# Unread TensorE products put into five waits of a one-core fp32 transformer chain

## The chip, the cores and the metric

The kernel runs on one core of one Trainium2 chip, as one program with one launch. The metric is the device time in microseconds (us), the median of several executions. One further execution is recorded by the hardware profiler; all rows below are from that one.

## The reference

A first block and four layers work on x of 512 x 1024 in fp32, together with a context of 256 rows. Cut to what matters here:

```python
def first_block(x, p, ...):
    u = rms_norm(h, norm_mix_w[l])
    proj = u @ w_in[l]
    ...                                   # RG-LRU half ya, HGRN2 half yb
    h = h + jnp.concatenate([ya, yb], axis=-1) @ w_out[l]
    gate = jax.nn.sigmoid(rms_norm(h, ple_norm_w[l]) @ w_ple_gate[l] + b_ple_gate[l])
    h = h + gate * (p[l] @ w_ple_proj[l])
    return rms_norm(h, final_norm_w)

def second_block(x, c, ctx, ...):
    for i in range(4):                    # conv, RWKV, attention, conv
        shift, scale, gate = modulation(c, mod_w[i], mod_b[i])
        h = modulate(rmsnorm(x, norm_g[i]), shift[:, None], scale[:, None])
        ...                               # hc: the same for the context
        x = x + gate[:, None] * y         # y: the layer's mixer of h and hc
    return rmsnorm(x, final_g)

def rwkv_features(h, proj, with_out):
    xx = centred_shift(h) - h
    lerp = lambda n: h + xx * mu[n]
    k = lerp(2) @ w_k
    ...

def rwkv_readout(o, r, v, k_sum, g, r_k, ln_g, ln_b, w_o):
    ...                                   # group norm of o, bonus
    return (y * jax.nn.silu(g)) @ w_o
```

In the RWKV layer the features feed a recurrence over 768 rows (context, then x) in both directions, which the kernel computes in chunks of 64 rows.

## The kernel before, in words

Rows lie on the 128 partitions in tiles of 128; X holds 4 such tiles of x, XC 2 of the context. For a matrix product an operand is split into a high and a low part (`hi`, `lo`, or `whi`, `wlo` for weights), each in a reduced fp32 form, and three products are summed: hi·hi, hi·lo, lo·hi. ScalarE makes the high part of a weight (L170), VectorE the low part (L173). A norm makes tiles xn, TensorE transposes them against the identity (L261 in `normed_T`, L693 in the layers), and ScalarE reads the transposed tile with its scale and shift into h (L710). PSUM is in two pools: `pmm`, six banks named mm for sums, and `ptr`, two banks named tr for transposes.

The program is laid out ahead by a planner: it runs through the kernel's instructions in a simulated time, and so fixes the order of each engine's list. On the chip every engine works through its list in order, and waits on semaphores. Where the kernel says `manual_schedule`, the order is that of the program text; `high_priority` moves instructions forward in it.

Five places matter here. (1) The beginning: the input rows, the identity and the first vectors are loaded, `_load_cols` transposes the vectors (L157), `normed_T` makes four tiles xn (L256) and transposes them, and the first products with w_in follow (L199 to L202). (2) The end of the first block: `done_g` adds the bias to the gate's sum in PSUM (L556), takes the sigmoid of z in place (L557), multiplies z in place by the projection of p (L561) and adds it to X (L562); for the very last tile a small square root of one column of z (L560) loads ScalarE's table early. Norms of the result follow, and the first conv layer transposes with L693. (3) The entry of the RWKV layer: `lerped(first)` makes, for each of eight feature tiles k, the shifted difference xx (L1050), the interpolation l (L1041), and its halves lhi (L270, ScalarE) and llo (L273, VectorE), which the products L199 to L202 read. (4) The end of the recurrence: `chain_o` sums one chunk's outputs in two PSUM banks `s.ops` (L1459, L1466), ScalarE copies them to Os (L1469), a transfer writes them out (L1471), and the readout reads rows back into ro, norms them and transposes them (L1654). Pools are closed and opened between the two (`open_w(4)`). (5) The end of the RWKV layer: `linear_tm` of w_o (L218 to L220), whose results are added to X and XC (L721, L722), and then the attention layer's norm and its transposes (L693).

Of the kernel before, what the change touches and what calls it, by code (L numbers as in the profile page):

```python
# [10 lines left out]
F32 = mybir.dt.float32  # L11
F32R = mybir.dt.float32r
AF = mybir.ActivationFunctionType
# [5 lines left out]
P = 128  # L19
D = 1024  # L20
# [49 lines left out]
class K:  # L70
# [16 lines left out]
    def setup(self):  # L87
        nc, es = self.nc, self.es
        self.const = self.pool(es, "const")
        self.small = self.pool(es, "small", bufs=3)  # L90
        self.open_w(side="right")

        self.ident = self.const.tile([P, P], F32, name="ident")
        self.cols = self.const.tile([P, NCOL], F32, name="cols")
        self.eps6 = self.const.tile([P, 1], F32, name="eps6")
        nc.vector.memset(self.eps6, EPS)
        self.eps5 = self.const.tile([P, 1], F32, name="eps5")
        nc.vector.memset(self.eps5, 1e-5)
        self.inv_d = self.const.tile([P, P], F32, name="inv_d")
        nc.vector.memset(self.inv_d, 1.0 / D)  # L100
        self.eps12 = self.const.tile([P, 1], F32, name="eps12")
        nc.vector.memset(self.eps12, 1e-12)
        self.epsg = self.const.tile([P, 1], F32, name="epsg")
        nc.vector.memset(self.epsg, 256e-5)
        self.KC, self.KA, self.NK = KC_OFF, KC_OFF["ka"], KC_OFF["nk"]
# [19 lines left out]

    def open_ctx(self, **kw):
        return self.pool(self.ses, "streamc", **kw).tile([P, 2, D], F32, name="XC")

    def mm(self):

# [112 lines left out]
        return t  # L243


    def normed_T(self, X, gain, pool):

        nc = self.nc
        hi = pool.tile([P, KT, T], F32R, name="hT_hi")
        lo = pool.tile([P, KT, T], F32R, name="hT_lo")  # L250
        with self.tc.tile_pool(name="ntw", bufs=1) as work:
            rstd = self.rms_rstd(X, 4, work)
            xn = []
            for i in range(4):
                t = work.tile([P, D], F32, name="xn", bufs=4)
                nc.vector.tensor_scalar(t, X[:, i, :], rstd[:, i:i + 1], None, ALU.mult)  # L256
                xn.append(t)
            for k in range(KT):
                ps = self.ptr.tile([P, 512], F32, name="tr")
                for i in range(4):  # L260
                    nc.tensor.transpose(ps[:, i * P:(i + 1) * P], xn[i][:, k * P:(k + 1) * P], self.ident)  # L261
                g = self.col(gain, k)
                nc.scalar.activation(hi[:, k, :], ps, AF.Copy, scale=g)  # L263
                nc.vector.scalar_tensor_tensor(lo[:, k, :], ps, g, hi[:, k, :].bitcast(F32), ALU.mult, ALU.subtract)
        return hi, lo
# [9 lines left out]
    def first_block(self, X, XC):  # L275
        nc, ins = self.nc, self.ins
        with ExitStack() as es:
            big = self.pool(es, "fb")
            mix = big.tile([P, KT, T], F32, name="mix")
            with ExitStack() as es2:  # L280
                up = self.pool(es2, "fbu")
                with self.tc.high_priority(offset=10 * WPRIO):
                    uh, ul = self.normed_T(X, "norm_mix_w", up)
                with self.tc.tile_pool(name="colp1", bufs=1) as pool:
                    self._load_cols(pool, [(8, P)])
                self.silu_cols()
# [231 lines left out]
        with ExitStack() as es2:  # L518
            st = self.pool(es2, "ple")
            bg = self.bcast_row("bg", ins["b_ple_gate"].rearrange("o n -> (o n)"), st)  # L520
            nc.sync.dma_start(XC, ins["ctx_2"].rearrange("o (t p) n -> p (o t) n", p=P))
            p = st.tile([P, 4, 256], F32, name="p")
            nc.sync.dma_start(p, ins["p"].rearrange("o b (t q) n -> q (o b t) n", q=P))
            ph = st.tile([P, 2, T], F32R, name="ph")
            pl = st.tile([P, 2, T], F32R, name="pl")
            for k in range(2):
                ps = self.ptr.tile([P, 512], F32, name="tr")
                for i in range(4):
                    nc.tensor.transpose(ps[:, i * P:(i + 1) * P], p[:, i, k * P:(k + 1) * P], self.ident)
                nc.scalar.activation(ph[:, k, :], ps, AF.Copy)  # L530
                nc.vector.tensor_tensor(pl[:, k, :], ps, ph[:, k, :].bitcast(F32), ALU.subtract)
            pp = st.tile([P, 4, D], F32, name="pp")
            w_pp = ins["w_ple_proj"].rearrange("o k n -> (o k) n")
            for nh in range(2):
                self.linear_tm(w_pp, nh * 512, lambda k: ph[:, k, :], lambda k: pl[:, k, :], TILES,
                               lambda j, t, ps, nh=nh: nc.scalar.activation(pp[:, j, nh * 512:(nh + 1) * 512], ps, AF.Copy),
                               kts=2)
            gh, gl = self.normed_T(X, "ple_norm_w", st)

            rsc, rs1, rs2 = [self.const.tile([P, 4], F32, name=n) for n in ("rsc", "rs1", "rs2")]  # L540
            for t in range(2):
                junk = st.tile([P, D], F32, name="junk")
                nc.scalar.activation(junk, XC[:, t, :], AF.Square, scale=1.0 / 32.0, accum_out=rsc[:, t:t + 1])
            self.rsqrt(rsc[:, 0:2], rsc[:, 0:2], self.eps6)


            fw = self.bcast_row("fw", ins["final_norm_w"], st)
            s1, s2 = [st.tile([P, 4, 2], F32, name=n) for n in ("s1", "s2")]
            warm = st.tile([P, 1], F32, name="warm")
            w_pg = ins["w_ple_gate"].rearrange("o k n -> (o k) n")  # L550
            for nh in range(2):
                def done_g(j, t, ps, nh=nh):
                    ns = slice(nh * 512, (nh + 1) * 512)
                    z = st.tile([P, 512], F32, name="z", bufs=2)
                    x = X[:, j, ns]
                    nc.vector.tensor_tensor(z, ps, bg[:, ns], ALU.add)  # L556
                    nc.scalar.activation(z, z, AF.Sigmoid)  # L557
                    if nh and j == 3:

                        nc.scalar.activation(warm, z[:, 0:1], AF.Sqrt)  # L560
                    nc.vector.tensor_tensor(z, z, pp[:, j, ns], ALU.mult)  # L561
                    nc.vector.tensor_tensor(x, x, z, ALU.add)  # L562
                    junk = st.tile([P, 512], F32, name="sqj", bufs=2)
                    nc.scalar.activation(junk, x, AF.Square, scale=1.0 / 32.0, accum_out=s1[:, j, nh:nh + 1])
                    nc.vector.tensor_tensor(x, x, fw[:, ns], ALU.mult)
                    junk = st.tile([P, 512], F32, name="sqj", bufs=2)
                    nc.scalar.activation(junk, x, AF.Square, scale=1.0 / 32.0, accum_out=s2[:, j, nh:nh + 1])
                self.linear_tm(w_pg, nh * 512, lambda k: gh[:, k, :], lambda k: gl[:, k, :], TILES, done_g, last=1 + nh)
            nc.vector.tensor_tensor(rs1, s1[:, :, 0], s1[:, :, 1], ALU.add)
            nc.vector.tensor_tensor(rs2, s2[:, :, 0], s2[:, :, 1], ALU.add)  # L570
            nc.vector.tensor_scalar(rs1, rs1, EPS, None, ALU.add)
            nc.vector.scalar_tensor_tensor(rs2, rs1, EPS, rs2, ALU.mult, ALU.add)
            for r in (rs2, rs1):
                nc.scalar.activation(r, r, AF.Sqrt)
                nc.vector.reciprocal(r, r)
            self.pre = (rsc, rs2, rs1)
# [385 lines left out]
    def rwkv_layer(self, X, XC):  # L962
# [82 lines left out]
        def lerped(n, first=False):  # L1045
            his, los = [], []
            for k in range(KT):
# [3 lines left out]
                his.append(lerp.tile([P, WH], F32R, name="lhi"))  # L1051
                los.append(lerp.tile([P, WH], F32R, name="llo"))
                lerp_k(n, k, his[k], los[k])
            return (lambda k: his[k]), (lambda k: los[k])


# [392 lines left out]
        def chain_o(j, part):  # L1449
# [12 lines left out]
            if j:  # L1462
                for p in range(NP):
                    for hh in range(2):
                        for d in range(2):
                            nc.tensor.matmul(f64(s.ops[hh])[hs[d], p, :], s.AR[d][hs[hh], p, 1, :], S[j % 2][hs[hh], d, p, :],  # L1466
                                             start=False, stop=p == NP - 1)
            for hh in range(2):
                nc.scalar.activation(s.Os[:, hh::2, :], f64(s.ops[hh]), AF.Copy)  # L1469
            for d in range(2):  # L1470
# [159 lines left out]
            nc.sync.dma_start(y_d[t * P:(t + 1) * P, :], buf[0])  # L1630
        es.close()
        self.open_w(4)


        X, XC = self.open_stream(side="right"), self.open_ctx(side="right")
        with ExitStack() as es:
# [26 lines left out]
            for nh in range(2):  # L1663
                nsl = slice(nh * 512, (nh + 1) * 512)

                def done(j, t, ps, nsl=nsl):
# [3 lines left out]
                    else:  # L1670
                        self.residual(work, gates[1], X, j - 2, nsl, ps)

                self.linear_tm(ins["rwkv_w_o_2"][0], nh * 512, lambda k: hi[:, k, :], lambda k: lo[:, k, :],
                               [t * P for t in early + late], done, last=1 + nh * (LG - 1))
        return X, XC


# [321 lines left out]
def build(tc, ins, out, taps=None, stages="F0123", test=None):  # L1999
    k = K(tc, ins, taps)  # L2000
    nc = tc.nc
    with k.es:
# [3 lines left out]
        with tc.high_priority(offset=10 * WPRIO):  # L2006
            for t in range(4):
                nc.sync.dma_start(X[:, t, :], ins["x"][0, t * P:(t + 1) * P, :])
            nc.sync.dma_start(k.ident, ins["ident"])
            with tc.tile_pool(name="colp0", bufs=1) as pool:  # L2010
                k._load_cols(pool, [(0, 8)])
        k.silu_c()
        if "F" not in stages:
# [58 lines left out]
```

## Time and profile before

| what | value |
|---|---|
| median of 3 runs | 2657.45 us (2656.79 to 2659.92) |
| profiled execution | 2661.63 us |
| its span, first to last instruction | 2659.7 us |
| mean granted clock of TensorE over the span | 0.935 |

The profiled execution's time holds its span and what lies around it. The granted clock is a share of TensorE's full speed: 1.00 is the level of 2.4 GHz and 0.50 that of 1.2 GHz, and a mean between the two is a stretch with both in it.

### The profile page before, as it was taken

What the parts mean: (1) busy time and instruction counts of PE and PEld (TensorE: products, weight loads), DVE (VectorE), ACT (ScalarE), POOL (GpSimd) and SP (SyncE); (2) the same over time, 40 slices, a digit from 0 to 9 for tenths busy, and PEclk for the clock granted to TensorE, in tenths of its full rate; (3) what the DMA queues carried; (4) which work ended last, traced back from release to release, by engine and by line L of the source; (5) the groups of instructions that cost most, each with busy time, mean ns of one, the idle gap of its engine ahead of it and who ended that gap; (6) DMA issues with size and microseconds to landing.
All of it is one profiled execution on the core that took longest, in us unless ns stands there. A gap on an engine that the chain in (4) does not pass through costs nothing. (4 is left out here: it accounts for less than half of the span.)

```text
span 2659.7 us, 48444 instructions
## 1 busy us (share of the span) xinstructions
PE 2388.7 (90%) x19868; PEld 1889.9 (71%) x19868; DVE 1653.5 (62%) x2580; ACT 1096.2 (41%) x2029; POOL 589.7 (22%) x544
## 2 busy tenths in 40 slices
PE   6998889899896889998799886989999899997997
PEld 4786667777575767666678775768788788876655
DVE  4434366995456478888788773554163478448836
ACT  4642353111434456653455552243233467432223
POOL 0101001000204046654232441110000387100001
PEclk8998899899997999997899997989999999998998
DMA  6533543434322237775433445242545311222331
GB/s 170 150 88 103 158 128 87 106 96 119 90 74 79 76 115 224 212 218 173 139 129 130 146 137 191 103 129 87 152 148 153 119 48 41 80 87 72 88 97 56
DMA packets 352941, 319.05 MB, mean 120 GB/s; under 512 B 19679, under 2 KB 292032, under 8 KB 352208
## 3 DMA queue, kind: packets, MB, share of 16 engines
q1 hardware_dynamic: 352720, 315.95, 39.6%
q8 instruction: 157, 2.57, 0.4%
q14 instruction: 64, 0.52, 0.1%
HBM read 241.85 MB, written 64.63 MB: 115 GB/s over the span
## 5 line engine op out<-in xcount | busy, mean ns | idle before, releaser
L173 DVE TENSOR_TENSOR wlo<-wraw,whi 128x1024 fp32r<-128x1024 f32 x212 | 263.6, 1244 | 460.9 <-ACT whi L170 453.4
L170 ACT ACTIVATE whi<-wraw 128x1024 fp32r<-128x1024 f32 x212 | 224.2, 1058 | 644.0 <-PE mm L200 336.0
L200 PE MATMUL mm<-hT_lo,whi 128*128 128x512 f32 (+1 forms) x864 | 323.5, 375 | 0.0
L199 PE MATMUL mm<-hT_hi,whi 128*128 128x512 f32 (+1 forms) x864 | 319.5, 381 | 2.5 <-ACT h L710 1.0
L202 PE MATMUL mm<-hT_hi,wlo 128*128 128x512 f32 (+1 forms) x864 | 290.7, 372 | 0.4 <-DVE wlo L173 0.4
L837 DVE SCALAR_TENSOR_TENSOR cvo<-ypad,dwh,cvo 128x784 f32<-128x784 f32 (+1 forms) x270 | 236.7, 906 | 4.7
L202 PEld LDWEIGHTS mm<-hT_hi,wlo 128*128 128x128 f32 x864 | 164.0, 190 | 40.6 <-issue 2.0
L199 PEld LDWEIGHTS mm<-hT_hi,whi 128*128 128x128 f32 x864 | 164.7, 191 | 38.6 <-issue 12.8
L200 PEld LDWEIGHTS mm<-hT_lo,whi 128*128 128x128 f32 x864 | 164.5, 191 | 32.7 <-issue 5.4
L218 PE MATMUL mm<-whi,hT_hi 128*128 128x512 f32 x384 | 152.6, 398 | 1.3 <-ACT hT_hi L263 1.3
L219 PE MATMUL mm<-wlo,hT_hi 128*128 128x512 f32 x384 | 152.3, 397 | 0.0
L220 PE MATMUL mm<-whi,hT_lo 128*128 128x512 f32 x384 | 150.1, 399 | 0.0
L797 POOL MEMSET ypad<- 128x15 f32 x16 | 1.8, 114 | 494.5 <-DVE cvo L837 272.1
L200 PE MATMUL mm<-llo,whi 128*128 128x256 f32 (+1 forms) x256 | 89.7, 368 | 11.3 <-DVE llo L273 11.3
L199 PE MATMUL mm<-lhi,whi 128*128 128x256 f32 (+1 forms) x256 | 85.0, 369 | 6.2 <-ACT lhi L270 6.2
L218 PEld LDWEIGHTS mm<-whi,hT_hi 128*128 128x128 f32 x384 | 72.5, 189 | 18.4 <-issue 1.8
L1317 ACT ACTIVATE Df<-ps 32x128 f32<-32x128 f32 x176 | 68.2, 387 | 37.9 <-PE ps L1310 35.7
L218 PE MATMUL mm<-whi,lhi 128*128 128x512 f32 x192 | 80.2, 424 | 4.0 <-DVE so L1566 3.2
L219 PEld LDWEIGHTS mm<-wlo,hT_hi 128*128 128x128 f32 x384 | 72.5, 189 | 15.6 <-issue 1.0
L220 PEld LDWEIGHTS mm<-whi,hT_lo 128*128 128x128 f32 x384 | 71.8, 189 | 16.5 <-issue 2.4
L613 PE MATMUL tr<-mraw,sc 128*32 128x128 f32 x1536 | 67.4, 291 | 16.8 <-DMA mraw<-in_mod_w_dram 13.6
L219 PE MATMUL mm<-wlo,lhi 128*128 128x512 f32 x192 | 79.9, 416 | 1.8 <-DVE wlo L173 1.8
(523 smaller groups left out, 5822.1 us busy)
## 6 DMA issues: line engine op xcount, KB each, us to landing
mraw<-in_mod_w_dram SPq DMA_DIRECT2D x96, 512.0 KB
wraw<-in_conv_w_in_dram SPq DMA_DIRECT2D x48, 512.0 KB
wraw<-in_attn_w_in_dram SPq DMA_DIRECT2D x48, 512.0 KB
wraw<-in_w_in_dram SPq DMA_DIRECT2D x24, 512.0 KB
f_d<-F SPq DMA_DIRECT2D x32, 384.0 KB
ar_d<-AR SPq DMA_DIRECT2D x32, 384.0 KB
F<-f_d SPq DMA_DIRECT2D x24, 512.0 KB
AR<-ar_d SPq DMA_DIRECT2D x24, 512.0 KB
```

The lines of the kernel that those rows point to most:

```text
L170: nc.scalar.activation(hi[:, :n], raw, AF.Copy)
L173: nc.vector.tensor_tensor(lo[:, :n], raw, hi[:, :n].bitcast(F32), ALU.subtract)
L199: nc.tensor.matmul(ps[s], wh[:, k, :], xh(k)[:, a:b], start=k == 0, stop=False)
L200: nc.tensor.matmul(ps[s], wh[:, k, :], xl(k)[:, a:b], start=False, stop=False)
L202: nc.tensor.matmul(ps[s], wl[:, k, :], xh(k)[:, a:b], start=False, stop=k == kts - 1)
L218: nc.tensor.matmul(ps, h, wh[:, kk, :], start=k == 0, stop=False)
L219: nc.tensor.matmul(ps, h, wl[:, kk, :], start=False, stop=False)
L220: nc.tensor.matmul(ps, l, wh[:, kk, :], start=False, stop=k == kts - 1)
L613: nc.tensor.matmul(ps[g:g + 32, 0:P], self.sc[:, k, :], raw[:, k, :], start=k < 4, stop=k >= 4)
L797: nc.gpsimd.memset(yp_[:, 0:15], 0.0)
L837: nc.vector.scalar_tensor_tensor(acc, yp_[:, tap:tap + W], dwh[:, tap, kt:kt + 1], acc, ALU.mult, ALU.add)
L1317: nc.scalar.activation(s.Df[rows, :, :, gsl].rearrange("p t a u -> p u a t"), p3[rows, :, 32 * b:32 * b + 32].rearrange("p u (a t) -> p u ...
```

## The change

A new method `warm(n, x)` takes a bank from `ptr` and issues n products of a constant tile (`inv_d`, 128 x 128, all 1/1024) with x into it; nothing reads the bank. It is called with 22 products of `inv_d` with itself at the beginning, where TensorE's order is now that of the text; with four products after each of the four tiles xn of the first norm; with 28 products that read z, between L560 and the multiplication L561; with four products on each of the eight lhi tiles of the RWKV layer's entry; with 60 products on a new constant tile wz behind the recurrence; and with 16 products that read the end of X's first tile behind the RWKV layer. wz is filled by a new ScalarE copy of 64 columns of `s.ops[0]` in the last chunk, ahead of the two copies to Os. That makes 22 + 16 + 28 + 32 + 60 + 16 = 174 products and one copy. Nothing is removed.

```diff
+        self.wz = self.const.tile([P, 64], F32, name="wz")
...
+    def warm(self, n, x):
+
+        ps = self.ptr.tile([P, 512], F32, name="tr")
+        for _ in range(n):
+            self.nc.tensor.matmul(ps[:, 0:x.shape[1]], self.inv_d, x, start=True, stop=True)
...
-    def normed_T(self, X, gain, pool):
+    def normed_T(self, X, gain, pool, warm=False):
...
                 nc.vector.tensor_scalar(t, X[:, i, :], rstd[:, i:i + 1], None, ALU.mult)
                 xn.append(t)
+                if warm:
+                    self.warm(4, t[:, 0:P])
...
-                    uh, ul = self.normed_T(X, "norm_mix_w", up)
+                    uh, ul = self.normed_T(X, "norm_mix_w", up, True)
...
                         nc.scalar.activation(warm, z[:, 0:1], AF.Sqrt)
+                    if nh and j == 3:
+                        self.warm(28, z[:, 0:P])
                     nc.vector.tensor_tensor(z, z, pp[:, j, ns], ALU.mult)
...
                 lerp_k(n, k, his[k], los[k])
+                if first:
+                    self.warm(4, his[k][:, 0:P].bitcast(F32))
...
+            if j == 11:
+                nc.scalar.activation(self.wz, s.ops[0][:, 0:64], AF.Copy)
             for hh in range(2):
                 nc.scalar.activation(s.Os[:, hh::2, :], f64(s.ops[hh]), AF.Copy)
...
         self.open_w(4)
+        self.warm(60, self.wz)
...
                                [t * P for t in early + late], done, last=1 + nh * (LG - 1))
+            self.warm(16, X[:, 0, D - P:])
...
-            with tc.tile_pool(name="colp0", bufs=1) as pool:
+            with tc.tile_pool(name="colp0", bufs=1) as pool, tc.manual_schedule(engines={mybir.EngineType.PE}):
+                k.warm(22, k.inv_d)
                 k._load_cols(pool, [(0, 8)])
```

## Rows read from the trace of the kernel before

**Rows 1.** The page, part 1: busy us, share of the span, instructions.
```profile
PE 2388.7 (90%) x19868; PEld 1889.9 (71%) x19868; DVE 1653.5 (62%) x2580; ACT 1096.2 (41%) x2029; POOL 589.7 (22%) x544
```

**Rows 2.** Windows: length, busy us of each engine, PEclk (granted clock), DMA share, GB/s.
```profile
386.00:387.00 1.00, 0.00 (x0) 0.00 (x0) 1.00 (x2) 1.00 (x3) 0.00 (x0) 0.86 0.86 243
387.00:388.00 1.00, 0.00 (x0) 0.00 (x0) 0.51 (x1) 0.98 (x3) 0.00 (x0) 0.50 0.76 202
400.00:401.00 1.00, 0.64 (x3) 0.21 (x2) 0.00 (x0) 1.00 (x2) 1.00 (x2) 0.81 0.00 0
...
803.00:836.00 33.00, 17.29 (x54) 12.07 (x52) 30.09 (x27) 11.81 (x18) 24.00 (x11) 0.59 0.11 31
...
1639.00:1640.00 1.00, 0.00 (x0) 0.00 (x0) 0.00 (x0) 0.00 (x0) 0.00 (x0) 0.71 0.89 246
1731.00:1732.00 1.00, 0.00 (x0) 0.00 (x0) 1.00 (x2) 0.00 (x0) 0.00 (x0) 0.79 0.46 43
```

**Rows 3.** Timeline of TensorE (start, us, what), small products elsewhere in the kernel.
```profile
188.99 1.16 PE L477 MATMUL tr<-qs,enb 128*128 128x128 f32 x8
...
377.38 0.83 PE L623 MATMUL tr<-msel,mrow 128*128 128x2 f32 x6
```

**Rows 4.** Timeline, the beginning; brackets hold the idle time before and its releaser.
```profile
0.96 0.17 DVE L100 MEMSET inv_d<- 128x128 f32 x1
...
9.81 0.24 PE L157 MATMUL tr<-ident,rows 8*128 8x8 f32 x1 [9.81 <-DMA rows<-in_norm_mix_w_dram]
...
17.16 0.63 PE L200 MATMUL mm<-hT_lo,whi 128*128 128x512 f32 x1
17.59 0.63 PE L199 MATMUL mm<-hT_hi,whi 128*128 128x512 f32 x1
...
46.06 0.48 PE L157 MATMUL tr<-ident,rows 128*128 128x128 f32 x2 [2.52 <-DMA rows<-in_conv_dw_dram]
```

**Rows 5.** Timeline of TensorE, VectorE and ScalarE, end of the first block.
```profile
384.15 0.40 PE L219 MATMUL mm<-wlo,hT_hi 128*128 128x512 f32 x1
...
384.39 0.39 PE L220 MATMUL mm<-whi,hT_lo 128*128 128x512 f32 x1
...
385.84 0.61 ACT L557 ACTIVATE z<-z 128x512 f32<-128x512 f32 x1
...
388.67 0.69 DVE L561 TENSOR_TENSOR z<-z,pp 128x512 f32<-128x512 f32 x1 [1.17 <-ACT warm L560]
...
393.92 0.93 PE L693 MATMUL mm<-ident,xn 128*128 128x128 f32 x2 [9.14 <-DVE xn L684]
...
394.44 3.53 DVE L684 TENSOR_SCALAR xn<-X,rs 128x1024 f32<-128x1024 f32 x4
...
395.25 4.96 PE L693 MATMUL mm<-ident,xn 128*128 128x128 f32 x22 [0.40 <-DVE xn L684]
...
399.60 1.45 ACT L710 ACTIVATE h<-mm,mod,gs 128x512 f32<-128x512 f32 x2 [2.85 <-PE mm L693]
```

**Rows 6.** Timeline, the last halves and products of the RWKV layer's first interpolation.
```profile
832.65 1.96 DVE L273 TENSOR_TENSOR llo<-l,lhi 128x770 fp32r<-128x770 f32 x2
...
835.27 0.51 PE L202 MATMUL mm<-lhi,wlo 128*128 128x256 f32 x2
```

**Rows 7.** Timeline of TensorE and ScalarE, end of the recurrence and the readout.
```profile
1634.73 1.16 PE L1466 MATMUL ps<-S,AR 64*64 64x64 f32 x64
...
1635.97 1.09 ACT L1469 ACTIVATE Os<-ps 128x512 f32<-128x512 f32 x2 [3.45 <-PE ps L1466]
...
1647.12 1.94 PE L1654 MATMUL tr<-ident,ro 128*128 128x128 f32 x8 [11.23 <-DMA ro<-y_d]
...
1671.27 0.50 PE L218 MATMUL mm<-whi,ry_hi 128*128 128x512 f32 x1 [1.00 <-ACT ry_hi L1657]
```

**Rows 8.** Timeline of TensorE, from the RWKV layer to the attention layer.
```profile
1729.15 0.39 PE L220 MATMUL mm<-whi,ry_lo 128*128 128x512 f32 x1
...
1735.59 0.45 PE L693 MATMUL mm<-ident,xn 128*128 128x128 f32 x1 [6.05 <-issue]
```

## Prediction, made before the change was run

> **What bounds the kernel now.** I read the page's busy shares first, then one-microsecond windows around the idle stretches of TensorE, then TensorE's timeline at each of the five places the edit touches. TensorE is busy for 90% of the span [rows 1]; every other engine stays under 65% in the same view. So TensorE sets the pace over most of the kernel, and its time has two prices. The profile's time table gives a mean granted clock of 0.935; the level seen in the low stretches is 0.50, that is 1.2 of 2.4 GHz [rows 2], so about (1 − 0.935)/0.5 = 13% of the span, some 346 us, runs at the low level. The reader should see in [rows 2] when it falls. At 386 to 387 the mean is 0.86, so (0.86 − 0.5)/0.5 = 0.7 of that microsecond ran high and the fall came at about 386.7; the last product had ended at 384.78 [rows 5]: 1.9 us of idling. Behind the RWKV layer it fell at about 1731.6, 2.0 us after TensorE's last product [rows 2, 8]; behind the recurrence at about 1639.4, 3.5 us after [rows 2, 7]. It rose at about 400.4 [rows 2], after transposes that had run since 393.92 [rows 5]. So the question at each place is whether products that nobody reads leave the clock high at the moment when the next needed product starts, and what stands behind them meanwhile.
>
> **The price of one product.** At the low level 22 products of 128 columns take 4.96 us [rows 5] and 8 take 1.94 [rows 7]: (4.96 − 1.94)/14 = 0.216 us each. Half of it at the high level is 0.108; 8 at that level in 1.16 us, [rows 3], is 7 × 0.108 and a tail of 0.40, so it fits. Six products with 2 columns take 0.83 [rows 3], which with a tail of 0.3 is 0.106 each: fewer columns save nothing, so the columns are not what a small product waits for. The 60 products of 64 columns therefore cost what 128 columns do. 174 products are added: 19 us at the high level, 38 at the low one, nearly all of it inside waits.
>
> **The beginning (22 + 16 products).** The fill of the weight tile ends at 1.13 us and TensorE's first instruction stands at 9.81 [rows 4], so 22 × 0.216 = 4.8 us end at about 6, with 3.8 us of idling behind them. In [rows 2] that much idling lets the clock fall. The four after each normalised tile are the part that bears: they fill the gaps between the first transposes. The gain is bounded by the low stretch itself: 512-column products follow each other at 0.43 us [rows 4] where 0.24 is the high level's distance [rows 5]; seven such before 18 us are 7 × 0.19 = 1.3, with the transposes 1.5. The loss is bounded by one group in front of needed transposes, 4 × 0.216 = 0.9, and a little for the two banks that they share. What comes early here is partly lost again: at 46.06 TensorE waits 2.52 us for a transfer [rows 4], whose start follows the DMA queue and not TensorE. I take −0.4, with −1.5 and +1.2 as ends.
>
> **Behind the first block (28 products).** Here the edit adds a true wait. The products read z, and the multiplication at L561 writes z in place, so VectorE must wait for the last of them. z is ready at 385.84 + 0.61 = 386.45; L561 started at 388.67, held by ScalarE's own read of z [rows 5]. At the high level 28 × 0.108 = 3.0, so the products end at 389.5 and L561 is 0.8 late. At the low level they take 6.05, end at 392.5, and it is 3.8 late. The products begin 0.3 before the fall seen in [rows 2], so both levels may be seen; I take +2.0. What is queued behind L561 on VectorE, in this order, is the sum into X, its product with the final norm's gain, the small operations of the normalisation, then the tiles xn whose transposes start at 393.92 [rows 5]: one queue and one chain, so the delay passes through whole. And the idle time from L561 to those transposes, 393.92 − 388.67 = 5.25 us, stays as long as it was. In [rows 2] idling of 1.9 to 3.5 us brings the low level, so the transposes would begin low as before. If they did not, 22 of them would be limited by xn, made until 394.44 + 3.53 = 397.97 [rows 5], and h would start near 398.2 instead of 399.60: −1.4; and the dense products behind would not begin low, another −1.6 as an estimate (eight 512-column ones at 0.2). Ends: +3.8 and 0.8 − 3.0 = −2.2.
>
> The Trainium skill, "TensorE: Matmul & The Clock Gate", Part 4, says that the full clock does not engage for transposes, since they don't count as busy in the same way. The trace differs: the clock rose at 400.4 with nothing but transposes behind it, in [rows 2, 5]. By the page, ordinary products would be what a stretch of transposes lacks, and this place would come out at its end of −2.2; by the rows the transposes raise it alone.
>
> **In front of the RWKV layer (32 products).** From 803 to 836 TensorE is busy for 17.3 of 33 us and VectorE for 30.1, at a mean clock of 0.59 [rows 2]. VectorE sets the time; four products of 0.86 us in front of each group fit into TensorE's waits. Only the last two groups count: the last low half ends at 832.65 + 1.96 = 834.6 and TensorE finishes its share at 835.8 [rows 6]. Four more products late in that row cost up to 0.9; a clock raised a little earlier saves up to 0.3, since only the last pairs follow the last low half, and 1.2 us lie between them. I take +0.2.
>
> **Behind the recurrence (one copy, 60 products).** ScalarE copies 64 columns into wz ahead of the two copies to Os. The copies to Os begin at 1635.97, right behind TensorE's last product, and the two take 1.09 [rows 7]; a copy of 64 columns lies between nothing and half of that, by its size nearer 0.25. It delays Os, the write of it, and with it the release of the pools on which the loads of ro depend: +0.3. The products start when the PSUM banks are free, about 1637.4, and end at 1643.9 (60 × 0.108) or 1650.4 (60 × 0.216). The next needed product waits for a transfer until 1647.12 [rows 7]. So the cover holds at the high level; at the low one they would end 3.3 late. If the clock then stayed high up to 1653, up to 3 us of TensorE's time would be saved, but at 1671.27 it waits 1.00 us for ScalarE's copy [rows 7], which hangs on the group norm and not on TensorE; what comes early there only waits longer. I take +0.3, ends −1.0 and +3.3.
>
> **Behind the RWKV layer (16 products).** 16 × 0.108 = 1.7 or, at the low level, 3.5 us, in an idle stretch of 6.05 [rows 8]. At worst nothing is late. At 1731.3 TensorE idles again for over 4 us, longer than the 2.0 after which it fell [rows 2]. I take 0, with −1.6 if the products behind 1735.59 start high (estimated like the stretch behind the first block).
>
> **Sum.** −0.4 + 2.0 + 0.2 + 0.3 + 0 = +2.1 us. The profiled execution took 2661.63 (span 2659.7 and 1.93 around it), 4.18 above the median of the three runs; on its own scale it becomes 2663.7. With the same difference on the median, 2657.45 + 2.1 = 2659.55; I forecast **2659.5**. About 0.2%, 5.3 us, can be told from no change, so this is no change.
>
> **Rivals.**
> *The clock is held.* The products leave the level high when the needed work starts. For it: the fall comes 1.9 to 3.5 us after work ends, so it is not immediate, and shifting the last product later by 3 to 6 us moves the fall. Against it: 5.25, 3.5 and over 4 us of idling remain behind three groups. Sum of the ends: −1.5 − 2.2 − 0.3 − 1.0 − 1.6 = −6.6, so 2650.9. Chance 0.25; in about four fifths of it the gain is over 5.3.
> *The products run at the low level throughout* and so outlast their waits. This ends on the other side. The price is 0.216 instead of 0.108 at every place: +3.8 behind the first block, +3.3 + 0.3 behind the recurrence, +0.9 in front of RWKV, +0.9 at the beginning, 0 behind RWKV: +9.2, so 2666.6. It decides as soon as the clock stands at 0.50 in the windows of 387 to 392 and 1638 to 1647. For it: each group starts 1.5 us or more into an idle stretch. Against it: at two of the places it starts before the clock fell in [rows 2]. Chance 0.17, nearly all of it over 5.3.
> *Another order.* The order on each engine is laid out ahead by the planner, which now places 174 products and a copy more. A needed product or a weight split may change places far from the edits. The waits in these rows are 0.4 to 6 us long, so one or two such shifts are ± 6 us. Chance 0.11, equally to both sides, half of it beyond 5.3.
> *The forecast* has the remaining 0.47.
>
> **How the numbers follow.** Faster by over 0.2%: four fifths of 0.25 and 0.03 of the order, and 0.02 from the forecast's low ends: 0.25. Slower: 0.16, 0.03 and 0.02: 0.21. Within: 0.54. The range takes in both rivals down to about a tenth on each side: 2649 to 2667. The forecast's own range is 2655 to 2663.
>
> **What would show it.** Right: VectorE's L561 one to four us later, released by TensorE; the transposes behind it still at 0.2 us each; the first needed transposes behind the recurrence at 1647 plus the shift; the mean clock hardly higher. Wrong: windows at full clock from 393 to 400 or from 1735 to 1741 (the first rival), a release by the unread products at ro's transposes (the second), or the gain or loss in a stretch that no edit touches (the third).

## The result, and the profile after

The changed kernel takes 2686.22 us (median of 4 runs, 2685.26 to 2689.62), against 2657.12 in the same comparison: ratio 1.0115, 95% interval 1.0099 to 1.013. It is 29 us slower, far outside the forecast's range. Its profiled execution took 2689.62 us with a span of 2687.9, 28.2 over the span of before, so one pair of traces shows nearly the whole difference. The mean granted clock is 0.933 against 0.935: the 174 products have not bought a higher clock.

Page of the changed kernel, part 1, as [rows 1]:

```profile
PE 2433.5 (91%) x20216; PEld 1939.5 (72%) x20216; DVE 1654.0 (62%) x2580; ACT 1094.3 (41%) x2030; POOL 587.9 (22%) x544
```

The first number to read is the count. TensorE's records rose from 19868 to 20216, by 348 = 2 x 174: each unread fp32 product is issued as two passes, each with its own weight load. The groups of `warm`'s line by form (count, shortest, median and longest pass in ns, first and last start) say so place by place:

```profile
L134 PE MATMUL tr<-wz,inv_d x120: 275/421/423, 1649.4 to 1673.4; 128*128 128x64 f32 x120
...
L134 PE MATMUL tr<-z,inv_d x56: 275/275/377, 390.6 to 396.8; 128*128 128x128 f32 x56
```

Where the time went shows when each TensorE instruction of the changed kernel is set against the same instruction of before (k-th start of the same source line). This table is worked out from the two traces' starts, as medians over 25 us, in us late; the columns to the right are four experiments of the next section. Each column sets one execution against one. For tile_alone of the next section, which has before's instructions in before's order and before's time, the same working gives between +1.0 and −5.0 along the trace and −2.2 at its end, and before's recorded execution (2661.63) lies 4.5 above its median. So a shift of a few us that grows slowly, above all in the recurrence from 875 to 1575, says little; a step at one place, with its wait in the trace, says more.

```
us in before   all five   start   block   front   behind
 100             +1.9     +3.6    -0.8    +0.9    +0.1
 350             +4.1     +2.3    -0.9    +1.0     0.0
 450             +8.7     +0.8    +3.6    -0.5    +0.3
 875             +9.5     +0.9    +6.4    +1.9    +0.1
1575             +7.5     -1.4    +5.1    +3.6    -5.8
1625            +13.0     +1.5   +11.3   +10.0    -5.8
1700            +27.5     +2.7   +12.1    +9.4   +11.3
2650            +28.1     +2.2   +15.7   +11.3   +16.8
```

Three steps carry the loss: 4.5 us behind the first block, some 5 near 1600, where no product stands, and 15 behind the recurrence. The beginning gives 2, and 2 more come at 304, where TensorE waits 8.4 us for the transfer of p instead of 6.4.

**Behind the first block** (timeline of the changed kernel, as [rows 5]):

```profile
390.57 6.52 PE L134 MATMUL tr<-z,inv_d 128*128 128x128 f32 x56 [1.73 <-ACT z L566]
...
397.19 0.69 DVE L572 TENSOR_TENSOR z<-z,pp 128x512 f32<-128x512 f32 x1 [5.62 <-PE tr L134]
```

The 28 products are 56 passes and last 6.5 us at the high level. The multiplication of z is released by the last of them, and starts 8.5 us later in the span than L561 did, of which 4.1 were lost earlier. The windows behind it show that nothing is got in return (length, busy us of each engine, granted clock, DMA share, GB/s):

```profile
400.00:402.00 2.00, 0.00 (x0) 0.00 (x0) 1.42 (x6) 1.02 (x4) 0.48 (x9) 0.94 0.00 0
402.00:405.00 3.00, 2.16 (x8) 1.60 (x9) 3.00 (x8) 0.86 (x2) 1.19 (x1) 0.50 0.00 0
```

The clock fell in the idle time that still follows, and the transposes begin at 0.50 as before.

**Behind the recurrence** (timeline and windows, as [rows 7]):

```profile
1649.41 24.43 PE L134 MATMUL tr<-wz,inv_d 128*128 128x64 f32 x120 [1.29 <-ACT Os L1484]
1673.63 1.92 PE L1670 MATMUL tr<-ident,ro 128*128 128x128 f32 x8
```

```profile
1650.00:1651.00 1.00, 1.00 (x11) 1.00 (x11) 0.00 (x0) 0.00 (x0) 0.00 (x0) 1.00 0.59 131
1651.00:1652.00 1.00, 1.00 (x7) 1.00 (x7) 0.00 (x0) 0.00 (x0) 0.00 (x0) 0.51 0.96 213
...
1660.00:1673.00 13.00, 13.00 (x63) 13.00 (x62) 4.31 (x4) 2.42 (x3) 4.69 (x2) 0.50 1.03 413
```

The 120 passes begin at the high level, fall to 0.50 after 1.6 us, and stay there for 22 us though TensorE never pauses. They hold up ro's transposes, which came 11.2 us after the end of the recurrence's products and now come 25.5 after it. But they are not what TensorE waits for last. ScalarE's list now has two squares and two roots of the group norm in front of the copies ry_hi (before has the first four of these copies in front of the first square), and the first square waits for GpSimd (ScalarE, then TensorE):

```profile
1667.09 1.06 ACT L1246 ACTIVATE ro<-ro 128x1024 f32<-128x1024 f32 x1 [17.73 <-POOL ro L1243]
...
1676.80 1.06 ACT L1673 ACTIVATE ry_hi<-tr 128x512 fp32r<-128x512 f32 x2
...
1677.43 0.80 PE L225 MATMUL mm<-whi,ry_hi 128*128 128x512 f32 x1 [1.89 <-ACT ry_hi L1673]
```

The transposes are done at 1675.5, and the first product with ry_hi still waits 1.9 us for ScalarE. Two things lie side by side here, the low level and ScalarE's list, and the list ends last.

**Near 1600** (timeline of ScalarE and TensorE; first the kernel before, then the changed one):

```profile
1591.47 1.09 ACT L1425 ACTIVATE G<-ps 128x512 f32<-128x512 f32 x2 [3.50 <-PE ps L1421]
...
1599.65 1.05 ACT L1233 ACTIVATE rx<-rx 128x1024 f32<-128x1024 f32 x1
...
1602.20 1.06 ACT L1435 ACTIVATE UV<-ps 64x512 f32<-64x512 f32 x2
...
1609.65 1.06 ACT L170 ACTIVATE whi<-wraw 128x1024 fp32r<-128x1024 f32 x1 [3.65 <-DMA wraw<-in_rwkv_w_o_dram]
```

```profile
1606.90 1.06 ACT L1246 ACTIVATE rx<-rx 128x1024 f32<-128x1024 f32 x1 [11.46 <-POOL rx L1243]
...
1609.45 1.06 ACT L1438 ACTIVATE G<-ps 128x512 f32<-128x512 f32 x2
...
1616.23 1.06 ACT L177 ACTIVATE whi<-wraw 128x1024 fp32r<-128x1024 f32 x1 [5.71 <-DMA wraw<-in_rwkv_w_o_dram]
1617.19 0.57 ACT L1448 ACTIVATE UV<-ps 64x512 f32<-64x512 f32 x1
...
1610.09 3.60 PE L1446 MATMUL ps<-G,CX 64*64 64x64 f32 x64 [3.52 <-ACT G L1438]
...
1617.82 0.48 PE L1456 MATMUL ps<-UV,BK 128*64 128x64 f32 x2 [4.01 <-ACT UV L1448]
```

Before, ScalarE copied G as soon as its products were done, and took the square and the root of a group norm (rx, gnr) later. In the changed kernel the planner has put both in front of G in ScalarE's list. The square waits for GpSimd, and G, whose products ended at 1599.4, waits behind it. A second exchange follows at once: the high half of a weight (whi), which waits 5.71 us for its transfer, now stands in front of the copy UV, which stood in front of it before. TensorE waits 3.5 us for G and 4.0 for UV.

### The profile page after: what moved, and what is told of

Read it like the earlier page. It is cut to its first block, busy times and chain, and to the rows that moved or that the text cites. A ratio compares the mean times of both kernels' runs of the same rounds, so it can differ in the third digit from the quotient of the medians.

```text
span 2687.9 us, 49135 instructions
## 1 busy us (share of the span) xinstructions
PE 2433.5 (91%) x20216; PEld 1939.5 (72%) x20216; DVE 1654.0 (62%) x2580; ACT 1094.3 (41%) x2030; POOL 587.9 (22%) x544
## 5 line engine op out<-in xcount | busy, mean ns | idle before, releaser
L207 PE MATMUL mm<-llo,whi 128*128 128x512 f32 (+1 forms) x256 | 87.1, 360 | 5.0 <-DVE llo L282 5.0
L206 PE MATMUL mm<-lhi,whi 128*128 128x512 f32 (+1 forms) x256 | 82.4, 360 | 3.5 <-ACT lhi L279 2.9
L624 PE MATMUL tr<-mraw,sc 128*32 128x128 f32 x1536 | 69.0, 293 | 15.3 <-DMA mraw<-in_mod_w_dram 12.1
```

The lines of the kernel that those rows point to most:

```text
L206: nc.tensor.matmul(ps[s], wh[:, k, :], xh(k)[:, a:b], start=k == 0, stop=False)
L207: nc.tensor.matmul(ps[s], wh[:, k, :], xl(k)[:, a:b], start=False, stop=False)
L624: nc.tensor.matmul(ps[g:g + 32, 0:P], self.sc[:, k, :], raw[:, k, :], start=k < 4, stop=k >= 4)
```

## The experiments

Ratios are to the kernel before on the same chip, with the 95% interval; they differ from the quotient of the two medians by up to 0.001. The kernel before had medians between 2656.4 and 2658.5 us in the five comparisons.

**Each place alone** (the changed kernel with the other places' lines taken out):

> The kernel before with the products of the beginning alone (22, and 4 behind each normalised tile); the other four places are as before. Two-pass theory (each unread fp32 product is issued as two passes, so it costs twice what the prediction said, and the loss lies where the products stand): TensorE's first needed work about 3 us late near 10 us, 1.9 us of it left at 100 us, no change behind that: 2659 us, between 2658 and 2661. Order theory (the added instructions make the planner lay out another order far from the edit, and that sets the time): TensorE's shift against the kernel before changes by several us at places far from the beginning, in the features, the recurrence or the readout, and the total lies outside 2656 to 2662.

> The kernel before with the 28 products behind the first block alone. Two-pass theory: the multiplication of z starts 4.5 us later than before, released by the last unread product (28 x 0.23 = 6.4 us instead of 3.0); that delay stays to the end: 2661.5 us, between 2660 and 2663. Order theory: the same delay, but further shifts of several us behind 900 us, total outside 2659 to 2664.

> The kernel before with the 32 products in front of the RWKV layer alone. Two-pass theory: about +1 us at 840 and no change behind: 2658 us, between 2657 and 2660. Order theory: shifts of several us between 900 and 1600, total outside 2656 to 2661.

> The kernel before with the copy to wz and the 60 products behind the recurrence alone. Two-pass theory: the products take about 24 us at the granted clock 0.50 and outlast the wait for ro by some 14 us: 2672 us, between 2670 and 2675, with no shift over 1 us in front of 1600. Order theory: a good part of the 20 us that the changed kernel loses between 1595 and 1680 is not the products' but that of work in another order: either the shift already starts in front of the products, or the total is under 2668.

> The kernel before with the 16 products behind the RWKV layer alone. They end inside the wait of 6 us (16 x 0.23 = 3.7), and ScalarE's lists near 1600 and in the readout are those of the kernel before: 2657.4 us within 2 by every theory that looks at those two lists and at the products' own length. If any other order of the rest costs several us: over 2661.

| run | median us | ratio (interval) |
|---|---|---|
| only_start | 2667.53 | 1.0038 (1.0024 to 1.0051) |
| only_block | 2673.10 | 1.0058 (1.0044 to 1.0073) |
| only_front | 2673.03 | 1.0058 (1.0044 to 1.0071) |
| only_behind | 2681.52 | 1.0087 (1.0073 to 1.0101) |
| only_end | 2659.17 | 1.0006 (0.9996 to 1.0016) |

Four of the five lose more than the two-pass theory expected, and by their ratios the four losses sum to 64 us where all places together cost 29. So they share a loss. The table of lateness shows one: only_block and only_front have the step of 6 to 7 us near 1600, far from their edits, with both exchanges in ScalarE's list; only_behind has neither. only_start has the square alone in front of G, and a step of 2 to 3. The order theory holds for only_block and only_front; the two-pass theory holds for the local part of only_block, whose products run at the low level from 0.4 us after their start:

```profile
385.56 8.15 PE L133 MATMUL tr<-z,inv_d 128*128 128x128 f32 x56 [1.73 <-ACT z L565]
...
393.81 0.69 DVE L571 TENSOR_TENSOR z<-z,pp 128x512 f32<-128x512 f32 x1 [7.25 <-PE tr L133]
```

The surprise is in only_behind. Its trace loses 22 us between 1640 and 1660, and none of it by the low level:

```profile
1631.34 13.61 PE L134 MATMUL tr<-wz,inv_d 128*128 128x64 f32 x120 [1.29 <-ACT Os L1480]
1644.79 1.04 PE L1666 MATMUL tr<-ident,ro 128*128 128x128 f32 x8
1660.25 0.79 PE L225 MATMUL mm<-whi,ry_hi 128*128 128x512 f32 x1 [14.42 <-ACT ry_hi L1669]
...
1649.91 1.06 ACT L1242 ACTIVATE ro<-ro 128x1024 f32<-128x1024 f32 x1 [18.62 <-POOL ro L1239]
...
1659.62 1.06 ACT L1669 ACTIVATE ry_hi<-tr 128x512 fp32r<-128x512 f32 x2
```

Here the same 120 passes ran at the high level and were done in 13.6 us. The transposes were done at 1645.8, and then TensorE waited 14 us for ScalarE, whose list has two squares and two roots of the group norm in front of the copies ry_hi. It is the list of the changed kernel. With one product, or with transposes, in place of the 60 products (behind_one, behind_tr) the first four copies stand in front again; so it seems that the planner had reckoned TensorE busy and filled ScalarE with what was free by its own times. The square in fact waits for GpSimd.

**Order, without the products' length.**

```diff
 tile_alone:     before, and only
+        self.wz = self.const.tile([P, 64], F32, name="wz")
 behind_one, block_one, front_one, start_one:  the place alone, and
-        for _ in range(n):
+        for _ in range(1):
 behind_tr, block_tr, front_tr, all_tr:  the place alone (all five), and
-            self.nc.tensor.matmul(ps[:, 0:x.shape[1]], self.inv_d, x, start=True, stop=True)
+            self.nc.tensor.transpose(ps[0:x.shape[1], 0:P], x, self.ident)
```

> The kernel before with the constant tile wz declared, and nothing that fills, reads or multiplies it: no instruction is added, but the memory layout shifts by 256 bytes and the planner lays out another order. Far-order theory (another order alone, anywhere, costs time): outside 2654 to 2659 us, by up to 10 us. Local theories (what the products themselves do where they stand): as before, 2656.4 within 2 us.

> As only_behind (copy to wz, products behind the recurrence), with 1 product instead of 60. The order up to the readout is that of only_behind; in the readout ScalarE's copies ry_hi stand in front of the group norm's squares again, as in the kernel before. Local theories (two passes, or the readout's order that follows from the planned length of the products): 2657 us, within 3 us of tile_alone. Far-order theory: within 5 us of only_behind's 2681.5.

> As only_front, with 1 product in place of each 4 in front of the RWKV layer: 8 products of two passes, under 2 us in all, in TensorE's waits. The planner still lays ScalarE's list near the recurrence's end as in only_front: the square and the root of a group norm stand in front of the copies G of the last chunks (in the kernel before they stand behind them). Order theory: TensorE loses 6 to 8 us at 1595 to 1605, and the total is 2664 to 2668 us. Product theory: as before, 2658.5 within 2.

> As only_front, with 4 transposes of each lhi tile in place of 4 products: 32 passes, twice as many as in front_one. Here ScalarE's list near 1600 is that of the kernel before (copies G in front of the group norm), where front_one and only_front have the other one. Order theory: no step of 6 to 7 us at 1600, and 2656 to 2660 us, under front_one although it has more passes. Pass theory: over front_one's 2661.6.

> As only_block, with 1 product instead of 28. ScalarE's list near the recurrence's end is that of the kernel before here. Order theory (only_block's 15 us are 4.5 us of products and the rest a group norm in front of the copies G): 2657 to 2661 us. If other differences of order count, it stays over 2664.

> As only_block, with 28 transposes of z in place of the 28 products: one pass each. ScalarE's list near the recurrence's end is that of the kernel before. Two-pass theory: 28 x 0.11 = 3.1 us at the high level, the multiplication of z starts 1 us late instead of 4.5 (up to 4 if the level is low): 2658 to 2662.5 us, and no step of several us at 1600. Rival (any 28 passes' worth of order change costs 10 us): over 2666.

> As only_start, with 1 product in place of the 22 and of each 4 behind a tile: 5 products, none of them late. ScalarE's list near 1600 has both copies G in front of the group norm. If only_start's 10 us are the time of its 38 products and of the transposes behind them: 2657 us within 2. If they come from the order laid out around them: over 2661.

| run | median us | ratio (interval) |
|---|---|---|
| tile_alone | 2658.10 | 1.0001 (0.9991 to 1.0011) |
| behind_one | 2660.29 | 1.0010 (1.0001 to 1.0019) |
| front_one | 2661.64 | 1.0014 (1.0003 to 1.0026) |
| front_tr | 2655.70 | 0.9991 (0.9979 to 1.0003) |
| block_one | 2657.02 | 1.0003 (0.9995 to 1.0012) |
| block_tr | 2667.86 | 1.0042 (1.0030 to 1.0053) |
| start_one | 2661.63 | 1.0011 (0.9999 to 1.0023) |

tile_alone does not test the order theory, against its expectation: by source line, operation and tile names its trace has the instructions of before in the order of before on every engine. front_tr refutes the wide form: 243 of VectorE's 2580 places in the list and 207 of ScalarE's 2029 hold another instruction than in before, and it is not slower. What costs are particular exchanges. behind_one and block_one, with one product each, lose next to nothing (1.0010 and 1.0003). front_one and front_tr are the cleanest pair. front_one has the fewer passes but both exchanges near 1600, and its lateness rises from −3.1 to +3.5 us across it; front_tr has twice the passes, G and UV in front, and stays at −7.4 and −7.3.

front_one's timeline, then front_tr's:

```profile
1596.42 1.06 ACT L1243 ACTIVATE rx<-rx 128x1024 f32<-128x1024 f32 x1 [11.57 <-POOL rx L1240]
1598.97 1.06 ACT L1435 ACTIVATE G<-ps 128x512 f32<-128x512 f32 x2
...
1605.74 1.06 ACT L176 ACTIVATE whi<-wraw 128x1024 fp32r<-128x1024 f32 x1 [5.70 <-DMA wraw<-in_rwkv_w_o_dram]
...
1599.60 3.68 PE L1443 MATMUL ps<-G,CX 64*64 64x64 f32 x64 [3.64 <-ACT G L1435]
...
1607.33 0.48 PE L1453 MATMUL ps<-UV,BK 128*64 128x64 f32 x2 [3.83 <-ACT UV L1445]
```

```profile
1583.36 1.09 ACT L1435 ACTIVATE G<-ps 128x512 f32<-128x512 f32 x2 [2.74 <-PE ps L1431]
...
1594.80 0.57 ACT L1445 ACTIVATE UV<-ps 64x512 f32<-64x512 f32 x1
...
1602.18 1.06 ACT L176 ACTIVATE whi<-wraw 128x1024 fp32r<-128x1024 f32 x1 [3.57 <-DMA wraw<-in_rwkv_w_o_dram]
...
1591.93 3.57 PE L1443 MATMUL ps<-G,CX 64*64 64x64 f32 x64
```

front_one's total missed its expectation by 2.4 us. Its trace is 3.1 us ahead in front of the step, but tile_alone's is ahead there too, by 2.4, so this may be chance. block_tr confirms the pass count where it acts:

```profile
386.84 3.28 PE L133 MATMUL tr<-ident,z 128*128 128x128 f32 x28 [1.73 <-ACT z L565]
...
390.22 0.69 DVE L571 TENSOR_TENSOR z<-z,pp 128x512 f32<-128x512 f32 x1 [2.39 <-PE tr L133]
```

28 single passes last 3.3 us, and the transposes behind are 1.2 us later than just ahead of the place. But its total is 10 us up, not the 0 to 5 expected: its lateness grows by small steps along the whole trace, and what makes them was not found. start_one does not settle the beginning: it lies between before and only_start, just over the 2661 that its expectation gave to the order, but its interval takes in 1.

**The products at the recurrence's end, with the order held.** behind_pinned takes the two engines' order in the readout's loop from the program text; behind_order writes out an order like that of before; behind_wide is behind_order with wz read twice.

```diff
 behind_pinned
+            with self.tc.manual_schedule(engines={mybir.EngineType.Activation, mybir.EngineType.DVE}):
                 for t in early + late:
 behind_order: in the same block, w = 0 loads or norms a tile, w = 1 transposes and copies it
+                for w, t in [x for t in early for x in ((0, t), (1, t))] + [(0, late[0]), (0, late[1]), (1, late[0]), (0, late[2]), (1, late[1]), (1, late[2])]:
 behind_wide
+    def warm(self, n, x, w=1):
...
+            self.nc.tensor.matmul(ps[:, 0:w * x.shape[1]].rearrange("p (w n) -> p w n", w=w), self.inv_d, x.unsqueeze(1).to_broadcast([P, w, x.shape[1]]), start=True, stop=True)
...
+        self.warm(60, self.wz, 2)
```

> As only_behind, with all 60 products, but with ScalarE's and VectorE's order in the readout's loop over tiles that of the program text: the ry_hi and ry_lo of the three early tiles come in front of the group norm of the late ones. Readout-order theory (the loss is ScalarE's copy ry_hi queued behind a square that waits for a transfer, 14.4 us in only_behind's trace): that wait shrinks under 3 us, the products' own end at 13.5 us behind their start delays ro's transposes by some 3 us at most, total 2656 to 2664 us. Two-pass theory (the products' own time in front of the transposes is the loss): within 4 us of only_behind's 2681.5.

> As only_behind, with 60 transposes of wz instead of 60 products: one pass each instead of two. The planned length halves, and ScalarE's order in the readout is that of the kernel before. Two-pass theory and readout-order theory: the 60 take 6.5 to 7 us at the high level (60 x 0.11) and end inside the wait for ro: 2656 to 2661 us. At the low level all the way 13 us, some 2 us outside the wait: 2659 to 2663. Far-order theory: over 2666.

> As only_behind, with all 60 products, and with ScalarE's and VectorE's order in the readout written out by hand after that of the kernel before: the copies of the three early tiles, then the group norms of two late tiles, the first one's copies, the third group norm, the other copies. (behind_pinned's text order freed the early copies but made one late group norm wait 13 us for the other.) Readout-order theory: 2656 to 2664 us, near 2659. Two-pass theory (the products' own time in front of ro's transposes is the loss): 2675 or more.

> As behind_order, with wz read twice by each of the 60 products, so 128 columns instead of 64; everything else is the same. In behind_order the 120 passes stayed at the granted clock 0.50 for all of their 24.7 us; in only_behind and behind_pinned the same passes stayed at 1.00 for 13.6 us. Column theory (back-to-back passes of 64 columns keep whichever level they begin at; passes of 128 raise it, as the 28 products of z did after 3 us): within 7 us of their start the clock stands at 1.00, the 60 end 14 to 18 us after their start, the total is 2660 to 2668 us. Rival (the level there depends on something else than the columns): some 24 us at 0.50 again, and 2672 to 2677 us.

| run | median us | ratio (interval) | the 120 passes in its trace |
|---|---|---|---|
| behind_pinned | 2683.68 | 1.0096 (1.0082 to 1.0110) | 13.6 us |
| behind_order | 2674.54 | 1.0069 (1.0057 to 1.0082) | 24.7 us |
| behind_wide | 2663.20 | 1.0033 (1.0020 to 1.0047) | 13.7 us |
| behind_tr | 2660.92 | 1.0011 (0.9999 to 1.0024) | 6.7 us (60 passes) |

behind_pinned's total falsified the expectation, its trace did not: the early copies no longer wait, but the text's order strings the late group norms one behind the other.

```profile
1647.36 1.09 ACT L1670 ACTIVATE ry_hi<-tr 128x512 fp32r<-128x512 f32 x2 [14.27 <-PE tr L1667]
...
1675.04 0.60 ACT L1670 ACTIVATE ry_hi<-tr 128x512 fp32r<-128x512 f32 x1 [13.08 <-PE tr L1667]
```

The first products with ry_hi are 1.4 us later than the work ahead of the 60 products (−2.65 against −4.03), where only_behind lost 22; the rest is lost at 1675. behind_order removes that wait too, and loses 14 us in another way, by the low level, which the changed kernel has beside its list:

```profile
1629.90 24.72 PE L134 MATMUL tr<-wz,inv_d 128*128 128x64 f32 x120 [1.29 <-ACT Os L1480]
1654.41 1.92 PE L1671 MATMUL tr<-ident,ro 128*128 128x128 f32 x8
```

```profile
1631.00:1632.00 1.00, 1.00 (x8) 1.00 (x7) 0.00 (x0) 0.00 (x0) 0.00 (x0) 0.60 1.04 213
...
1640.00:1650.00 10.00, 10.00 (x49) 10.00 (x48) 0.00 (x0) 0.00 (x0) 2.38 (x2) 0.50 1.03 414
```

With the order kept and 128 columns, behind_wide is 11 us faster than behind_order and stays at the high level throughout:

```profile
1632.60 13.66 PE L134 MATMUL tr<-wz,inv_d 128*128 128x128 f32 x120 [1.29 <-ACT Os L1480]
1646.10 1.04 PE L1671 MATMUL tr<-ident,ro 128*128 128x128 f32 x8
```

It had not fallen to the low level first, so the run shows the price of the level, 11 us of 24.7, and leaves the column theory untested. By the end of the passes its trace has lost 1.4 us, and 4.5 more by 1700; no run has this written order without the products, so what the order itself costs is not known.

**The whole, less a part.**

> The changed kernel without the copy to wz and the 60 products behind the recurrence; the other four places are left in. ScalarE's list still has the group norm in front of the copies G near 1600. If the places add up: the changed kernel's 2686 less 15 to 20, so 2666 to 2671 us, with a step of 6 to 7 us at 1600 and none at 1650. If what is lost elsewhere comes back in waits that the 60 products had covered: over 2675.

> The changed kernel with a transpose in place of each of the 174 products: half the passes. ScalarE's early copies in the readout stand in front again, the group norm near 1600 does not. Two-pass theory with the two lists: behind the first block 1 to 3 us instead of 4.5, behind the recurrence 0 to 3 instead of 15 to 20, the step of 6 to 7 us at 1600 stays: 2664 to 2672 us. If the number of passes is not what counts: over 2678.

no_behind takes 2674.51 us (1.0066, 1.0051 to 1.0080): the recurrence's products cost 12 of the 29, in the median, and four places with the step at 1600 (+6.9 in its trace) keep 17. That is 3.5 over the expected span. all_tr takes 2676.07 (1.0068, 1.0055 to 1.0082), 10 less than the changed kernel with half the passes, but 4 over its expected span. Up to 2050 its trace is 6.7 us late, as reckoned; another 10 are lost behind that, at 2100 and 2450 above all, where it differs from before only in order. At 2450 the trace shows most of it: VectorE runs 29 multiply-adds of the last conv (cvo) in a row ahead of TensorE's next products where before runs 24, and TensorE waits 18.85 us for them instead of 15.54. At 2100 no cause was found.

No version was faster than the kernel before by more than the comparison can tell; front_tr, the best, has an interval that takes in 1.

## Why the prediction was wrong

**The step that failed first is "The price of one product".** It took 0.216 and 0.108 us from [rows 3, 5, 7] as prices of products. The 22 and the 8 at the low level there are transposes, one pass each. The 8 at the high level [rows 3] were four products of two passes, and the "six products with 2 columns" three. So every count of the sum was half of what TensorE runs: 19 us at the high level should have been 38. The trace of before could have shown it: a line's count in the program against its count in the view.

**Behind the first block** I had 0.8 to 3.8 and took 2.0; two passes make it 28 × 0.216 = 6.0 us, so 3.8 at the high level. Measured: 4.5. The mechanism (z's anti-dependence, the whole chain behind it, no clock kept over the 5.25 us that follow) was right, and the size off by the pass count. The Trainium skill, "TensorE: Matmul & The Clock Gate", Part 4, says that the full clock does not engage for transposes. The trace does not agree: the transposes behind this place begin at 0.50, and the granted clock rises between 408 and 409 us (mean 0.71) after nothing but transposes since 402.4.

**Behind the recurrence** I took +0.3 with +3.3 as the end, for 13 us of products at most. They took 24.4, and the step is +15. Two things were wrong: the count, and the thought that a low level costs a few us more. With the right count the high level gives 13 us and about 1.4 late (behind_pinned's trace), the low one 24.4 and 14 late. And I had not looked for what the planner does while it thinks TensorE busy: in only_behind, with the products at the high level, ScalarE's list alone costs as much (17 us by 1700). The low level alone costs as much too (behind_order). The changed kernel has both, side by side, and the wait that ends last in it is that for ScalarE.

**In front of the RWKV layer** +0.2 was forecast and +0.9 measured (8.57 to 9.45 late). Small, and by the trace less than the passes' own length, as forecast. **Behind the RWKV layer** 0 was forecast, 0.5 measured, and only_end is not told from before. **At the beginning** −0.4 was forecast; the trace shows +1.9. The shift was gone at 25 to 40 us (0.0 late), but the transfers of later vectors then came later (3.51 us of waiting at 53.01), and the forecast had no term for that. Of the 10 us that only_start's ratio shows, its trace has 2.2; it is that of its fastest execution (2663.68, its median 2667.53). Where the rest lies is open.

**The rivals.** "The products run at the low level throughout" was the right side with 0.17, and too small for the same count. "Another order" had 0.11 and "± 6 us", and was nearest to the surprise: near 1600 it is +5 to +7 in six kernels, by the same two exchanges in ScalarE's list. I had priced it as noise of both signs, where it was the second mechanism, and had not asked which instruction of an in-order list waits longest if it comes early. **The total** is 1.9 + 2.2 + 4.5 + 0.9 − 2.0 (from 875 to 1575, about what tile_alone's trace has there) + 4.8 (to 1635) + 15.3 + 0.5 = 28.1 us.

**What stays open:** the 10 us of only_start and of block_tr beyond their places, all_tr's loss at 2100, what the two exchanges near 1600 cost each by itself, and why the level fell under the passes in the changed kernel and in behind_order, but not in only_behind and behind_pinned, which begin alike, 1.29 us after Os.

## What to carry to other kernels

Count what an instruction issues before pricing it: the records per product, not the products; a full fp32 product here is two passes, an fp32 transpose one. Filler work on one engine is also an entry in the planner's book: look at what it moves on the other engines' in-order lists, above all instructions that wait for a transfer and get in front of copies that are ready. And filler that ends before an idle stretch (5.25 us behind the first block) bought no clock here for what comes after it.

## What the runs showed of the hardware

TensorE stayed at the granted clock 0.50 for over 20 us while it ran 64-column fp32 passes without a pause (the changed kernel, 1652 to 1673; behind_order, 1632 to 1654), and at 1.00 for 13.6 us on the very same passes in only_behind and behind_pinned. The 128-column passes of z in only_block ran at 0.50 from 386 on, and at 1.00 from 390 to their end:

```profile
387.00:388.00 1.00, 1.00 (x7) 1.00 (x7) 0.00 (x0) 0.68 (x2) 0.00 (x0) 0.50 0.93 278
388.00:390.00 2.00, 2.00 (x14) 2.00 (x14) 0.00 (x0) 0.00 (x0) 0.00 (x0) 0.67 0.71 200
390.00:393.00 3.00, 3.00 (x30) 3.00 (x29) 0.00 (x0) 0.00 (x0) 0.00 (x0) 1.00 0.14 42
```

A pass of 64 columns took as long as one of 128: 13.6 us for 120 of either at the high level (only_behind, behind_wide). The Trainium skill, "FP8 and Floating Point Precision", TensorE Precision Notes, gives true FP32 four passes through the array. The trace does not agree: the records here show two per product, 348 for 174, and at 128 columns each takes the time of one transpose (6.5 us for 56, 3.3 for 28).
